# Differential attention's scores: from four products over 128 rows to three products over 64 rows for each map

## The chip, the cores and the metric

The kernel runs on one core of one Trainium2 chip. The metric is the device time of one execution in microseconds; the time before is the median of three runs. The core has five engines that work beside each other and meet at semaphores: TensorE (PE; the profile shows its weight loads apart, as PEld), VectorE (DVE), ScalarE (ACT), GpSimd (POOL) and SyncE (SP), whose queue issues nearly all DMA transfers here.

## The reference

One decoder layer over 1024 positions with a width of 1024: a norm, one wide projection (7184 columns), then two groups of heads side by side, eight of differential softmax attention and four of gated linear attention (GLA), then an output projection over both, a norm and the residual. All of it is float32. What the change touches is the first half of the differential attention:

```python
q = q * (DA_HEAD_DIM ** -0.5)                      # (B, S, 8 heads, 2 maps, 64)
s = jnp.einsum('bqhmd,bkhmd->bhmqk', qb, k)        # scores of two maps, each over 64 dimensions
mask = key_pos[None, :] <= q_pos[:, None]
p = jax.nn.softmax(jnp.where(mask, s, -jnp.inf), axis=-1)
w = p[:, :, 0] - lam * p[:, :, 1]
return jnp.einsum('bhqk,bkhv->bqhv', w, v)
```

A head has two maps, each with queries and keys of 64 dimensions; the weights are the difference of the two softmaxes, and the values have 128 dimensions.

## The kernel before

**Numbers in two parts.** Matrix products run on float32r operands, which keep fewer bits than float32. To hold the precision, an operand is split into a part rounded to float32r (hi) and the rest (lo), and a product is made of hi·hi, lo·hi and hi·lo. So most products in the kernel are three matmuls into one accumulation in PSUM, and each matmul (`mm`, L116) loads its own stationary operand. PE keeps the order in which the kernel writes matmuls and transposes (`keep_in_program_order`); a scheduler places the work of the other engines.

**Stages.** The input projection (`go`, `step`, L540 and L367) runs over pairs of column blocks with a seven-product scheme; GLA's work is fed in between (`fill`). Each finished block of 128 columns by 512 positions goes through `take` (L303), which splits q and k of a head into hi and lo (`qk_st`) and stores them in DRAM (L318). From about 650 us on three streams are merged (`merge`, L895 and L1290): the scores of all heads (`all_scores`, L991), the values (`all_values`, L1094) and the early part of the output projection (`out_early`, L1166, tiles `ypart`). Each stream gives each step a cost, and `merge` writes next the step of the stream that is furthest behind its line; so the order of matmuls on PE in this stage is fixed when the kernel is built. The last 60 us or so finish the output projection (`yps`).

**Scores before.** In DRAM, q and k of a head lie as `[map, part, 64, S]`. `load_qk` (L811) brings one half of the positions into an SBUF tile whose 128 rows are the 64 dimensions of the hi part above the 64 of the lo part, the two maps beside each other in the columns. For k there is a second tile, `ks`, with the parts swapped. A matmul of q with k over all 128 rows then gives hi·hi + lo·lo, and one of q with ks gives lo·hi + hi·lo: two matmuls make all four products of one map. `scores` (L944) does this for a block of 128 queries, for each map and for each part of up to 512 keys (`parts_of`, L922): `sc` is one of three PSUM banks, used in turn (`sc_bank`, L933); DVE reads it, adds the mask and keeps the minimum (L967; q is stored negated, so the minimum stands for the maximum); ACT takes the exponential (L975). After the second map DVE and POOL combine the two (L980 to L984). Blocks of queries go from the last to the first, so block 7 needs all keys and block 0 only 128 of them (a matmul has at least 256 columns).

**Loads before.** The tiles of the next head are loaded in the midst of a head (after block 4: the second half of q, both halves of k and ks) and at its end (the first half of q). The second halves have one buffer each, in which all heads follow each other; the first halves of k and ks alternate between two.

**Values.** `values` (L1006) turns the weights with PE transposes (`wtr`), splits them in two (`wt_hi`, `wt_lo`) and multiplies them with v (`po`).

Of the kernel before, what the change touches and what calls it, by code (L numbers as in the profile page):

```python
# [20 lines left out]
DA_HEADS = 8  # L21
# [10 lines left out]
def hymba_kernel(  # L32
# [50 lines left out]
    lam = const.tile([P, 1], F32, name="lam")  # L83
# [1 line left out]


    qk_d = {
        n: [tc.dram_tile([2, 2, 64, S], F32, name=f"{n}{h}_d") for h in range(DA_HEADS)]
        for n in "qk"
    }  # L90
    v_d = [tc.dram_tile([2, P, NT, P], F32, name=f"v{h}_d") for h in range(DA_HEADS)]
# [12 lines left out]
    def bank(i, shape, name):  # L104
        return psum.tile(shape, F32, tag=f"b{i}", name=name)
# [10 lines left out]
    def mm(*a, **k):  # L116
        tc.keep_in_program_order(pe.matmul(*a, **k))  # L117
# [35 lines left out]
    kp = ctx.enter_context(tc.tile_pool(name="kp", bufs=1))  # L153
# [39 lines left out]
    y, z = len(pairs) - 2, len(pairs) - 1  # L193
# [109 lines left out]
    def take(kind, n, half, unit, c):  # L303

        cs = cols(half)
        if kind in ("QA", "KA"):
            h = n + unit

            ending = made[0] > len(order) - LEAD
            tag, bufs = ("raw", 4) if ending and order[made[0] - 1][1] == 7 else ("st", 2)  # L310
            st = ap.tile([P, 2, 512], F32R, tag=tag, name="qk_st", bufs=bufs)
# [1 line left out]
            act.activation(st[:, 0], c, AF.Copy, scale=scale)  # L313
            dve.scalar_tensor_tensor(st[:, 1], c, scale, fp(st[:, 0]), ALU.mult, ALU.subtract)
            d = qk_d["q" if kind == "QA" else "k"][h]
            for m in range(2):
                rows = slice(64 * m, 64 * m + 64)
                ins = sp.dma_start(d[m, :, :, cs].rearrange("t p s -> p t s"), fp(st[rows]))  # L318
                if ending:
                    tc.keep_in_program_order(ins)  # L320
        elif kind == "VA":

            def sink(pt):
# [15 lines left out]
        elif kind in ("GA", "GB"):  # L339
# [5 lines left out]
            d = g_d[n + unit] if kind == "GA" else gg_d[n][unit]  # L345
            sp.dma_start(d[:, cs], g)
        elif kind == "QB":
            g = n + unit
            e_q, _ = decs[g]
            q = ap.tile([P, 2, 512], F32, tag="st", name="gq_st", bufs=2)  # L350
# [481 lines left out]
    for _ in fill[0] if fill else ():  # L832
        pass
    fill.clear()
    for n in ("q", "k", "ks"):
        load_qk(0, n, 1)
        if n != "q":
            load_qk(0, n, 0)
    load_qk(0, "q", 0)

    E, wo = D // P, {}
    md = mixd.rearrange("(e p) s -> p e s", p=P)
# [79 lines left out]
    def parts_of(n):  # L922
        return [(0, max(n, 256))] if n <= 512 else [(0, 512), (512, max(n, 768))]
# [9 lines left out]
    def sc_bank(name, shape):  # L933
        n_sc[0] += 1
        return bank(SC[n_sc[0] % 3], shape, name)
# [6 lines left out]
    w, used, scored = {}, set(), []  # L942

    def scores(h, qb):  # L944

        n = (qb + 1) * P
        qc = slice(qb % 4 * P, qb % 4 * P + P)
        st = const.tile([P, 6], F32, tag="stt", name="stt", bufs=4)
        p0 = pp.tile([P, n], F32, tag=f"p0_{qb}", name="p0", bufs=1)
        p1 = smp.tile([P, S], F32, tag="p1", name="p1", bufs=2)  # L950
        for m, p in enumerate((p0, p1)):
            q = qk[h, "q", qb // 4][:, m, qc]
            parts = parts_of(n)
            for i, (a, b) in enumerate(parts):
                sc = sc_bank("sc", [P, 512])
                for j, name in enumerate(("k", "ks")):
                    for half in range(2):
                        lo, hi = max(a, half * 512), min(b, half * 512 + 512)
                        if lo < hi:
                            mm(  # L960
                                sc[:, lo - a : hi - a], q,
                                qk[h, name, half][:, m, lo - half * 512 : hi - half * 512],
                                start=(j == 0), stop=(j == 1),
                            )
                e = min(b, n)
                last = i == len(parts) - 1
                dve.tensor_tensor_reduce(  # L967
                    p[:, a:e], sc[:, : e - a],
                    maskt[:, NZ + P - (e - a) :] if last else maskt[:, : e - a],
                    1.0, 3e38 if i == 0 else st[:, 4 + m : 5 + m], ALU.add, ALU.min,  # L970
                    st[:, m : m + 1] if last else st[:, 4 + m : 5 + m],
                )
# [6 lines left out]
                if last and m:  # L979
                    dve.reciprocal(st[:, 4:6], st[:, 2:4])  # L980
                    pool.tensor_scalar(  # L981
                        p1[:, :n], p1[:, :n], st[:, 5:6], lam, ALU.mult, ALU.mult
                    )
                    dve.scalar_tensor_tensor(  # L984
                        p0[:, :n], p0[:, :n], st[:, 4:5], p1[:, :n], ALU.mult, ALU.subtract
                    )
                    w[h, qb] = p0
                    c += 0.25 + n / 1024 * 1.4
                yield c

    def all_scores():  # L991
        for h in range(DA_HEADS):
            for qb in range(NT - 1, -1, -1):
                if qb % 2 and h:
                    yield lambda h=h, qb=qb: (h - 1, qb // 2) in used
                yield from scores(h, qb)
                if qb == 4 and h + 1 < DA_HEADS:
                    for n in ("q", "k", "ks"):
# [276 lines left out]
    def last_times(st, dh, part, e):  # L1275
# [8 lines left out]
    T = 8 * 36.0  # L1284
    LAG = 21.0
    s_cost = sum(
        2 * sum(0.08 + (min(b, n) - a) / 512 * 0.56 for a, b in parts_of(n)) + 0.25 + n / 1024 * 1.4
        for n in range(P, S + 1, P)
    )
    merge(  # L1290
# [119 lines left out]
```

## Time and profile before

| | us |
|---|---|
| median of three runs | 1022.69 |
| lowest, highest | 1018.75, 1025.47 |
| the profiled execution | 1019.5 |
| its span, first to last instruction | 1017.8 |
| mean granted TensorE clock | 0.997 |

The profile is of one execution. A group's row gives source line, engine, operation and the tiles (out<-in), the shape, the count, then busy time in us, the mean ns of one record, and the idle time of the engine just ahead of the group, with what ended it. All matmuls are written by the helper at L117 and all transposes by the one at L120, so they are told apart by their tiles: `sc` scores, `po` values, `wtr` turned weights, `ypart` and `yps` the output projection, `x`, `y`, `z` the input projection. Matmuls are pipelined, and the end of a matmul's record is modelled; starts are what to compare. SPq is the queue of SP, where DMA transfers are issued.

### The profile page before, as it was taken

The page shows a single profiled execution, that of the slowest core. Times are in us where ns is not written, and L with a number is a line of the kernel's source. Part 1 is how long each engine was busy: PE and PEld are TensorE (multiplying, and loading weights), DVE is VectorE, ACT ScalarE, POOL GpSimd, SP SyncE. Part 2 cuts the span into 40 slices and gives each one's busy share as a digit, 9 for nine tenths or more (in the row PEclk, how much of TensorE's full clock was granted, in tenths as well). Part 3 has the DMA queues.
Part 4 walks back from the last instruction along what each step waited for, and adds up shares of the span by engine and source line. Part 5 has one row for each costly group of instructions (what it writes and reads, how often), then busy time and mean ns, then how long its engine had stood idle before and what let it go on. Part 6 is the DMA issues. An engine that isn't in the chain of part 4 may idle for free.

```text
span 1017.8 us, 15017 instructions
## 1 busy us (share of the span) xinstructions
PE 981.8 (96%) x5006; PEld 823.2 (81%) x5006; DVE 727.6 (71%) x1486; ACT 606.1 (60%) x1208; POOL 133.2 (13%) x148
## 2 busy tenths in 40 slices
PE   4999999999999999999999999999999999999997
PEld 3777888887888878888888888778888887888765
DVE  5897866887667857867767765577777777777645
ACT  7754633684366635645567654356666667777664
POOL 6200000000001001000000000021231222343222
PEclk9999999999999999999999999999999999999999
DMA  9432435556867888888776647896566579975667
GB/s 333 153 87 87 136 123 189 181 173 223 258 226 240 259 258 273 273 281 267 247 254 193 189 155 250 280 368 222 185 217 195 198 268 374 273 187 82 164 192 149
DMA packets 145581, 220.39 MB, mean 217 GB/s; under 512 B 15216, under 2 KB 70512, under 8 KB 145408
## 3 DMA queue, kind: packets, MB, share of 16 engines
q1 hardware_dynamic: 141472, 212.09, 64.0%
q0 software_dynamic: 4032, 7.34, 4.8%
q8 instruction: 39, 0.64, 0.3%
q14 instruction: 38, 0.31, 0.1%
HBM read 133.93 MB, written 88.60 MB: 219 GB/s over the span
## 4 chain that ended last, share of the span: by engine, by line
PE 73%; DMA 10%; DVE 8%; issue 3%; ACT 2%; SPq 2%; POOL 0%; DVEq 0%; ACTq 0%
PE x L117 17%; PE z L117 11%; PE y L117 11%; PE ypart L117 10%; PE sc L117 5%; PE po L117 5%; PE yps L117 4%; DMA wo_d<-wo_raw 4%; PE wtr L120 2%; PE gpo L117 2%; DMA wo_raw<-in_w_out_dram 2%; DMA q_d<-qk_st 1%; DMA wo_hi<-wo_d 1%; PE vtr L120 1%; DVE w L259 1%
## 5 line engine op out<-in xcount | busy, mean ns | idle before, releaser
L975 ACT ACTIVATE p<-p,stt 128x896 f32<-128x896 f32 (+7 forms) x128 | 99.5, 777 | 49.4 <-DVE stt L967 44.6
L117 PE MATMUL y<-h_hi,w 128*128 128x512 f32 x448 | 114.0, 396 | 1.9 <-DVE s L510 1.0
L117 PE MATMUL x<-s_hi,w 128*128 128x512 f32 x448 | 112.5, 394 | 1.4 <-ACT s L373 1.4
L117 PE MATMUL z<-s_hi,w 128*128 128x512 f32 x448 | 113.6, 396 | 0.2 <-ACT s L373 0.2
L373 ACT COPY s<-x 128x512 f32<-128x512 f32 x84 | 49.0, 583 | 101.9 <-PE x L117 100.4
L258 ACT CAST w<-t 128x512 fp32r<-128x512 f32 x112 | 68.9, 621 | 62.0 <-PE y L117 30.1
L259 DVE TENSOR_TENSOR w<-t,w 128x512 fp32r<-128x512 f32 x112 | 76.6, 687 | 32.1 <-ACT w L258 31.6
L117 PEld LDWEIGHTS y<-h_hi,w 128*128 128x128 f32 x448 | 82.6, 188 | 19.4 <-ACT h_hi L466 2.1
L117 PEld LDWEIGHTS x<-s_hi,w 128*128 128x128 f32 x448 | 83.0, 188 | 18.6 <-ACT s L373 2.1
L117 PEld LDWEIGHTS z<-s_hi,w 128*128 128x128 f32 x448 | 82.4, 188 | 16.9 <-ACT s L373 0.6
L967 DVE CUSTOM_DVE_ANT_0 p<-sc,maskt 128x512 f32<-128x512 f32 (+3 forms) x128 | 74.8, 586 | 29.5 <-PE sc L117 28.5
L981 POOL TENSOR_SCALAR p<-p,stt,lam 128x1024 f32<-128x1024 f32 (+3 forms) x64 | 54.6, 854 | 277.4 <-DVE stt L980 155.2
L117 PE MATMUL ypart<-wo_hi,m_hi 128*128 128x512 f32 x192 | 79.6, 414 | 0.9 <-ACT yst L1163 0.8
L259 DVE TENSOR_TENSOR w<-w_raw,w 128x512 fp32r<-128x512 f32 x78 | 54.9, 704 | 32.6 <-ACT w L258 32.4
L117 PE MATMUL ypart<-wo_hi,m_lo 128*128 128x512 f32 x192 | 75.7, 394 | 0.0
L117 PE MATMUL ypart<-wo_lo,m_hi 128*128 128x512 f32 x192 | 75.5, 393 | 0.0
L729 POOL TENSOR_SCALAR_AFFINE_SELECT gan<-gan 128x512 f32<-128x512 f32 x8 | 10.7, 1336 | 484.1 <-ACT gan L728 484.1
L117 PE MATMUL sc<-k,q 128*128 128x512 f32 (+1 forms) x192 | 70.3, 369 | 1.9 <-DVE stt L967 1.9
L117 PE MATMUL sc<-ks,q 128*128 128x512 f32 (+1 forms) x192 | 66.2, 347 | 0.0
L258 ACT CAST w<-w_raw 128x512 fp32r<-128x512 f32 x78 | 48.1, 618 | 30.2 <-PE y L117 15.3
L384 DVE TENSOR_TENSOR c<-z,s 128x512 f32<-128x512 f32 x56 | 38.6, 688 | 35.6 <-ACT s L373 28.1
L984 DVE SCALAR_TENSOR_TENSOR p<-p,stt,p 128x1024 f32<-128x1024 f32 (+3 forms) x64 | 52.2, 816 | 16.1 <-POOL p L981 15.7
(202 smaller groups left out, 2250.5 us busy)
## 6 DMA issues: line engine op xcount, KB each, us to landing
w_raw<-in_w_in_dram SPq DMA_DIRECT2D x56, 512.0 KB, 5.5
wo_raw<-in_w_out_dram SPq DMA_DIRECT2D x32, 256.0 KB, 3.3
v_d<-v_st SPq DMA_DIRECT2D x32, 256.0 KB, 2.5
wo_d<-wo_hi SPq DMA_DIRECT2D x32, 256.0 KB, 2.4
wo_d<-wo_raw SPq DMA_DIRECT2D x32, 256.0 KB, 4.5
k_d<-qk_st SPq DMA_DIRECT2D x32, 256.0 KB, 4.5
q_d<-qk_st SPq DMA_DIRECT2D x32, 256.0 KB, 5.3
q<-q_d SPq DMA_DIRECT2D x32, 256.0 KB, 5.4
```

The costliest lines, as they stand in the source:

```text
L117: tc.keep_in_program_order(pe.matmul(*a, **k))
L120: tc.keep_in_program_order(pe.transpose(dst, src, ident))
L258: act.copy(w[:, 0], src)
L259: dve.tensor_tensor(w[:, 1], src, fp(w[:, 0]), ALU.subtract)
L373: act.copy(b[k], ps)
L384: dve.tensor_tensor(c, p0, p1, ALU.add)
L729: pool.affine_select(a, a, [[0, 4], [1, P]], ALU.is_ge, 0.0, base=0, channel_multiplier=-1)
L967: dve.tensor_tensor_reduce(p[:, a:e], sc[:, : e - a], maskt[:, NZ + P - (e - a) :] if last else maskt[:, : e - a], 1.0, 3e38 if i == 0 els ...
L975: act.activation(p[:, :n], p[:, :n], AF.Exp, bias=st[:, m : m + 1], scale=-1.0, accum_out=st[:, 2 + m : 3 + m],)
L981: pool.tensor_scalar(p1[:, :n], p1[:, :n], st[:, 5:6], lam, ALU.mult, ALU.mult)
L984: dve.scalar_tensor_tensor(p0[:, :n], p0[:, :n], st[:, 4:5], p1[:, :n], ALU.mult, ALU.subtract)
```

## The change

q and k lie in DRAM as `[part, 128, S]`: 64 rows of the first map above 64 rows of the second, with hi and lo apart, so that `take` stores a block with one transfer in place of two. In SBUF a tile has the two maps in the two halves of its rows and the two parts beside each other in the columns; the swapped tile `ks` is gone. A score is made of three matmuls with a contraction over 64 rows (hi·hi, lo·hi, hi·lo; lo·lo is left out), for both maps in turn, the first map on rows 0 to 63 and the second on rows 64 to 127, into two PSUM banks at once; then DVE reads the two banks. Each q and k tile is loaded with one transfer. Even heads use one set of four buffers and odd heads another, and all loads of the next head are issued after block 6, the second block of a head. The costs that `merge` goes by change with it: a step is now one part of both maps.

```diff
@@ take
-            for m in range(2):
-                rows = slice(64 * m, 64 * m + 64)
-                ins = sp.dma_start(d[m, :, :, cs].rearrange("t p s -> p t s"), fp(st[rows]))
-                if ending:
-                    tc.keep_in_program_order(ins)
+            ins = sp.dma_start(d[:, :, cs].rearrange("t p s -> p t s"), fp(st))
+            if ending:
+                tc.keep_in_program_order(ins)
@@ load_qk
-        if h % 2 and half == 0 and n != "q":
-            t = smps[0].tile([P, 2, 512], F32R, tag=f"{n}0", name=f"{n}0")
+        if h % 2 == 0:
+            t = kp.tile([P, 2, 512], F32R, tag=f"{n}{half}", name=f"{n}{half}")
+        elif n == "k":
+            t = kp.tile([P, 2, 512], F32R, tag=f"ks{half}", name=f"k{half}")
         else:
-            t = kp.tile([P, 2, 512], F32R, tag=f"{n}{half}", name=f"{n}{half}")
-        for m in range(2):
-            d = qk_d["q" if n == "q" else "k"][h][m, :, :, cols(half)]
-            if n != "ks":
-                sp.dma_start(fp(t[:, m]), d.rearrange("t p s -> (t p) s"))
-            else:
-                for i in range(2):
-                    sp.dma_start(fp(t[64 * i : 64 * i + 64, m]), d[1 - i])
+            t = smps[0].tile([P, 2, 512], F32R, tag=f"q{half}", name=f"q{half}")
+        sp.dma_start(fp(t), qk_d[n][h][:, :, cols(half)].rearrange("t p s -> p t s"))
@@ scores
-        for m, p in enumerate((p0, p1)):
-            q = qk[h, "q", qb // 4][:, m, qc]
-            parts = parts_of(n)
-            for i, (a, b) in enumerate(parts):
-                sc = sc_bank("sc", [P, 512])
-                for j, name in enumerate(("k", "ks")):
-                    for half in range(2):
-                        lo, hi = max(a, half * 512), min(b, half * 512 + 512)
-                        if lo < hi:
-                            mm(
-                                sc[:, lo - a : hi - a], q,
-                                qk[h, name, half][:, m, lo - half * 512 : hi - half * 512],
-                                start=(j == 0), stop=(j == 1),
-                            )
+        q = qk[h, "q", qb // 4]
+        parts = parts_of(n)
+        for i, (a, b) in enumerate(parts):
+            k, k0 = qk[h, "k", a // 512], a // 512 * 512
...
+            scs = [sc_bank("sc", [P, 512]) for _ in range(2)]
+            for j, (x, y) in enumerate(((0, 0), (1, 0), (0, 1))):
+                for m, sc in enumerate(scs):
+                    rows = slice(64 * m, 64 * m + 64)
+                    mm(
+                        sc[:, : b - a], q[rows, x, qc], k[rows, y, a - k0 : b - k0],
+                        start=(j == 0), stop=(j == 2),
+                    )
+            for m, (p, sc) in enumerate(zip((p0, p1), scs)):
                 dve.tensor_tensor_reduce(
...
-                c = 0.08 + (e - a) / 512 * 0.56
...
+            c = 0.16 + (e - a) / 512 * 0.9
@@ all_scores
-                if qb == 4 and h + 1 < DA_HEADS:
-                    for n in ("q", "k", "ks"):
-                        load_qk(h + 1, n, 1)
-                    for n in ("k", "ks"):
-                        load_qk(h + 1, n, 0)
-            if h + 1 < DA_HEADS:
-                load_qk(h + 1, "q", 0)
+                if qb == 6 and h + 1 < DA_HEADS:
+                    for n, half in (("q", 1), ("k", 0), ("k", 1), ("q", 0)):
+                        load_qk(h + 1, n, half)
```

More of the change, by code (lines that the diff above doesn't have):

```diff
@@ L87, in hymba_kernel @@
     qk_d = {
-        n: [tc.dram_tile([2, 2, 64, S], F32, name=f"{n}{h}_d") for h in range(DA_HEADS)]
+        n: [tc.dram_tile([2, P, S], F32, name=f"{n}{h}_d") for h in range(DA_HEADS)]
         for n in "qk"
@@ L834, in hymba_kernel @@
     fill.clear()
-    for n in ("q", "k", "ks"):
[L836 to L839, printed above, removed]
+    for n, half in (("q", 1), ("k", 0), ("k", 1), ("q", 0)):
+        load_qk(0, n, half)
     E, wo = D // P, {}
@@ L978, in scores @@
                     )
[L979 to L989, printed above, removed]
+            c = 0.16 + (e - a) / 512 * 0.9
+            if last:
+                dve.reciprocal(st[:, 4:6], st[:, 2:4])
+                pool.tensor_scalar(p1[:, :n], p1[:, :n], st[:, 5:6], lam, ALU.mult, ALU.mult)
+                dve.scalar_tensor_tensor(
+                    p0[:, :n], p0[:, :n], st[:, 4:5], p1[:, :n], ALU.mult, ALU.subtract
+                )
+                w[h, qb] = p0
+                c += 0.25 + n / 1024 * 1.4
+            yield c
     def all_scores():
@@ L996, in all_scores @@
                 yield from scores(h, qb)
-                if qb == 4 and h + 1 < DA_HEADS:
-                    for n in ("q", "k", "ks"):
-                        load_qk(h + 1, n, 1)
-                    for n in ("k", "ks"):
-                        load_qk(h + 1, n, 0)
-            if h + 1 < DA_HEADS:
-                load_qk(h + 1, "q", 0)
+                if qb == 6 and h + 1 < DA_HEADS:
+                    for n, half in (("q", 1), ("k", 0), ("k", 1), ("q", 0)):
+                        load_qk(h + 1, n, half)
         scored.append(True)
@@ L1286, in hymba_kernel @@
     s_cost = sum(
-        2 * sum(0.08 + (min(b, n) - a) / 512 * 0.56 for a, b in parts_of(n)) + 0.25 + n / 1024 * 1.4
+        sum(0.16 + (min(b, n) - a) / 512 * 0.9 for a, b in parts_of(n)) + 0.25 + n / 1024 * 1.4
         for n in range(P, S + 1, P)
```

4 lines of the change are left out of this document (2 added, 2 removed).

## The prediction

> **What bounds the kernel now.** I read the page from the top: busy time, the slices, then the chain that ended last.
>
> ```profile
> PE 981.8 (96%) x5006; PEld 823.2 (81%) x5006; DVE 727.6 (71%) x1486; ACT 606.1 (60%) x1208; POOL 133.2 (13%) x148
> PE   4999999999999999999999999999999999999997
> PE 73%; DMA 10%; DVE 8%; issue 3%; ACT 2%; SPq 2%; POOL 0%; DVEq 0%; ACTq 0%
> ```
>
> TensorE is busy for 96% of the span, in all slices but the first and the last, and holds 73% of the chain. A busy share says little of matmuls that overlap, so next I cut the stage that the change touches into windows (columns: window, length, then busy time of PE, weight loads, DVE, ACT and POOL, granted clock, DMA share, GB/s).
>
> ```profile
> 650.00:670.00 20.00, 17.71 (x82) 13.76 (x81) 14.12 (x38) 8.73 (x16) 3.27 (x3) 1.00 1.00 371
> 700.00:750.00 50.00, 49.87 (x292) 43.33 (x291) 37.40 (x103) 34.78 (x75) 12.00 (x13) 1.00 0.66 209
> 950.00:1018.00 68.00, 57.31 (x279) 46.21 (x277) 33.98 (x100) 38.37 (x108) 16.30 (x19) 0.98 0.68 167
> ```
>
> In the middle of the score stage PE has work for 49.87 of 50 us at the full clock, and DVE, the next, for 37.40: a microsecond taken from PE's stream there is a microsecond off the end. In the first 20 us the DMA engines are full (share 1.00), and in the last 68 PE waits for others.
>
> How many score matmuls there are, by shape (columns: operation, tile of the array, moving columns, count, busy us, ns of one record):
>
> ```profile
> L117 PE MATMUL sc<-k,q 128*128 128x512 f32 x96 | 40.1, 418 | 0.0
> L117 PE MATMUL sc<-ks,q 128*128 128x512 f32 x96 | 37.8, 393 | 0.0
> L117 PE MATMUL sc<-k,q 128*128 128x256 f32 x64 | 19.2, 302 | 0.5 <-DVE stt L967 0.5
> L117 PE MATMUL sc<-ks,q 128*128 128x256 f32 x64 | 17.9, 282 | 0.0
> L117 PE MATMUL sc<-k,q 128*128 128x384 f32 x32 | 11.4, 356 | 1.4 <-DVE stt L967 1.4
> L117 PE MATMUL sc<-ks,q 128*128 128x384 f32 x32 | 10.8, 338 | 0.0
> ```
>
> A record of 393 ns is not what a matmul costs: records overlap. The timeline gives the pitch, from one start to the next.
>
> ```profile
> 705.19 0.40 PE L117 MATMUL sc<-k,q 128*128 128x512 f32 x1
> 705.42 0.39 PE L117 MATMUL sc<-ks,q 128*128 128x512 f32 x1
> 705.65 0.39 PE L117 MATMUL ypart<-wo_hi,m_hi 128*128 128x512 f32 x1
> ...
> 716.46 0.33 PE L117 MATMUL sc<-k,q 128*128 128x384 f32 x1
> 716.63 0.34 PE L117 MATMUL sc<-ks,q 128*128 128x384 f32 x1
> 716.81 0.39 PE L117 MATMUL ypart<-wo_hi,m_hi 128*128 128x512 f32 x1
> ...
> 719.14 0.28 PE L117 MATMUL sc<-k,q 128*128 128x256 f32 x1
> 719.26 0.28 PE L117 MATMUL sc<-ks,q 128*128 128x256 f32 x1
> 719.38 0.40 PE L117 MATMUL po<-wt_hi,v 128*128 128x256 f32 x2
> ```
>
> So 0.23 us for 512 columns, 0.175 for 384, 0.12 for 256, and scores now take 192 x 0.23 + 64 x 0.175 + 128 x 0.12 = 44.2 + 11.2 + 15.4 = 70.8 us of PE's stream.
>
> **Part 1, the matmuls.** Two matmuls per map and part, over 128 rows, become three per map over 64 rows: 576 in 288 pairs (144 of 512 columns, 48 of 384, 96 of 256). Nothing in the trace uses half the rows, so the cost has two bounds. If the two of a pair stream together, a pair costs one pitch: 144 x 0.23 + 48 x 0.175 + 96 x 0.12 = 33.1 + 8.4 + 11.5 = 53.0 us, 17.8 less than now. If they stream one after the other, it is 106.0 us, 35.2 more. I take the first: the halves share no row, no weights and no PSUM bank, the order puts the two maps next to each other, and a record of 0.39 us beside a pitch of 0.23 shows that the array already holds two matmuls at once. But that is an argument and no measurement, and I keep both ends.
>
> The Trainium skill, "TensorE: Matmul & The Clock Gate", Part 3 on packing small matmuls, says that matmuls on different row groups run concurrently, their starts some 4 ns apart. No run here shows it yet; by it the 288 pairs would take, as an estimate, 1.2 us above the lower bound.
>
> **Part 2, weight loads.** Each of the 576 loads its own weights. Two rows bound a load's cost: short matmuls in a stream, and records of loads of 128 and of 64 columns.
>
> ```profile
> 399.82 1.78 PE gpo L117 x16
> ...
> L117 PEld LDWEIGHTS sc<-ks,q 128*128 128x128 f32 x192 | 36.4, 190 | 4.4
> ...
> L117 PEld LDWEIGHTS gkl_ps<-h_lo,wl 128*64 128x64 f32 x12 | 1.6, 135 | 1.2
> ```
>
> Sixteen matmuls of 128 columns take 1.78 us, 0.11 each; 64 more columns of weights take 190 - 135 = 55 ns, so 128 take 0.11: a load occupies its path for 0.11 us whatever streams. A pair needs two, 0.22 us one behind the other. That hides under 0.23, but not under 0.175 or 0.12. If the halves load side by side it costs nothing; if not, 144 narrower pairs take 0.22 and the sum is 33.1 + 31.7 = 64.8. I take nothing, since the halves have weight rows of their own, and keep +11.8 as the other end. The second matmul of a group can start behind the first by up to a load (0.11) or by nothing; once per group of six that is 0 to 10.6 us in 96 groups. I take 0.03, 2.9 us.
>
> **Part 3, changes of geometry.** In the built order of the changed kernel the score matmuls stand in 95 runs, with full-array matmuls between: 190 changes between 128 and 64 rows. The nearest rows are the low-rank product, which goes from 128 to 64 columns of the array in the midst of a stream.
>
> ```profile
> 77.88 0.62 PE L117 MATMUL z<-s_lo,w 128*128 128x512 f32 x2
> 78.33 0.85 PE L117 MATMUL gkl_ps<-s_hi,wl 128*64 128x512 f32 x3
> ...
> 81.33 0.85 PE L117 MATMUL gkl_ps<-h_lo,wl 128*64 128x512 f32 x3
> 82.01 0.63 PE L117 MATMUL z<-s_hi,w 128*128 128x512 f32 x2
> ```
>
> The last z starts at about 77.88 + 0.62 - 0.39 = 78.11 and the first gkl_ps 0.22 later; back at the end, 81.79 to 82.01, again 0.22. That is the plain pitch, so I take 0. The upper end is the array running empty, 0.39 - 0.23 = 0.16 us each, 30.4 us. The Trainium skill, "TensorEngine Tiling (Array Packing)", Key Properties, speaks against the change: a switch of tiling mode drains TensorE. The trace does not agree for columns (0.22 against a pitch of 0.23); for rows no run shows it. It is a rival below.
>
> **Part 4, PSUM banks.** Three banks rotate. A group now fills two at once, and DVE reads them one after the other.
>
> ```profile
> PE sc L117 <- DVE stt L967: 1.9, 2, 1.4
> L967 DVE CUSTOM_DVE_ANT_0 p<-sc,maskt 128x512 f32<-128x512 f32 (+3 forms) x128 | 74.8, 586 | 29.5 <-PE sc L117 28.5
> ```
>
> Now PE waits 1.9 us in all. With the pitches above laid along the built orders, before 3 reuses of a bank come less than 2 us of PE work after its last matmul; in the changed order 30 do, most at 1.3. A read takes 0.59 us, two 1.17, and DVE reads in its own order behind other work, so perhaps every third of the 30 is late by some 0.3 us: 3 us. PE takes its work in order: behind a score matmul that waits stand the ypart, wtr and po matmuls, and behind those the copies of ACT and DVE that empty them. Ends: 0, and 15 (each late by one read, 30 x 0.5). DVE and ACT do the same reads and exponentials as before.
>
> **Part 5, transfers.**
>
> ```profile
> L120 PE MATMUL vtr<-ident,c 128*128 128x128 f32 x128 | 18.3, 277 | 3.0 <-DVE c L384 3.0
> ...
> 358.83 6.13 DMA q_d<-qk_st
> 654.98 7.33 DMA q_d<-qk_st
> 662.37 9.48 DMA v<-v_d
> ...
> q<-q_d SPq DMA_DIRECT2D x32, 256.0 KB, 5.4
> k<-k_d SPq DMA_DIRECT2D x32, 256.0 KB, 5.8
> ks<-k_d SPq DMA_DIRECT2D x64, 128.0 KB, 6.1
> ```
>
> The ks loads go (64 x 128 KB = 8.4 MB of 220), and 128 load issues on SP become 32, 64 stores 32; the bytes stored stay. All of this lies beside a full PE but where the chain names a transfer: the q_d store at 358.83, and the q_d and v transfers at 655 to 672, with the DMA engines full. Loads a head earlier need no wait on SP, since their buffers were last read a head before; the v loads queue behind fewer of them. The stores cost SP issue time alone, beside a full PE. I take 2 us gained; ends 0 and 5, the second all that PE idles from 650 to 670 (20 - 17.71 = 2.3) and ahead of the vtr transposes (3.0, if that wait behind DVE's c is the store's at 358.83, whose buffer the next tile needs).
>
> **The sum**, against the profiled execution of 1019.5 us (span 1017.8): -17.8 + 0 + 2.9 + 0 + 3 - 2 = -13.9, so 1005.6. That execution lies 3.2 under the median of the runs, 1022.7; the forecast on that is 1009.
>
> **Rivals.**
> - *Pairs overlap, loads do not.* +11.8 on the sum: -2.1, so 1021. For it: 0.11 us per load in every stream shown. Against: separate rows.
> - *Each change of geometry drains the array.* Slower, from a point: 13.9 / 190 = 0.073 us per change. At 0.16 it is -13.9 + 30.4 = +16.5, 1039. For it: 190 changes, almost none adjacent. Against: the 0.22 of the low-rank product.
> - *The change does not do what it says:* the halves do not stream together. +35.2 on the matmuls, +3 for banks, -2 for transfers: +36, 1059; as PE is full, all of it lands on the end. For it: no row shows two streams in one array.
>
> **Chances.** Forecast 0.36 (its own range 1003 to 1013), loads in series 0.20, drain 0.19, no overlap 0.25. A measurement of this kernel tells about 1% (10 us) from no change. Faster by over 1%: nearly all of the forecast and the mild end of the drain, 0.36. Within 1%: loads in series, and the middle of the drain, 0.27. Slower: no overlap and the full drain, 0.37. The range reaches from 1003 to 1062, past the no-overlap case; only combinations of rivals lie above.
>
> **What would show it.** Starts of the two maps' score matmuls some 0.03 us apart and pairs 0.23 apart confirm part 1; single starts 0.23 apart refute it. Pairs of 256 columns at 0.12 or 0.22 settle part 2. The step into and out of a score run, above the pitch, settles part 3. The row of PE sc waiting for DVE stt should stay under 15 us, and ks gone from the list of DMA issues without PE waiting for q or k. The prediction is wrong above all if PE's time in the scores' stream rises instead of falling.

## The result, and the profile after

| | before | after |
|---|---|---|
| median, us | 1020.72 (4 runs, 1018.37 to 1025.47) | 1036.16 (4 runs, 1035.40 to 1037.17) |
| profiled execution | 1019.5 | 1036.62 |
| its span | 1017.8 | 1034.9 |

The ratio is 1.0146, with a 95% interval of 1.0104 to 1.0188: the changed kernel is 15 us slower, where the forecast was 1009. The time lies in the range and close to the rival in which each change of geometry drains the array (1039).

The page of the kernel after, its busy times and its chain of waits:

```profile
PE 1000.8 (97%) x5198; PEld 801.9 (77%) x5198; DVE 727.2 (70%) x1486; ACT 604.2 (58%) x1208; POOL 137.0 (13%) x148
PE 83%; DVE 6%; DMA 4%; ACT 4%; issue 3%; POOL 0%; DVEq 0%; SPq 0%; POOLq 0%; ACTq 0%
```

PE is busy for 19 us more (1000.8 against 981.8), the span is 17.1 us longer, and PE's part of the chain has grown from 73% to 83%. So the time was lost in PE's own work more than in waits for others; what it waited for comes further down. Next, where: the stage from the first score to the first `yps`, as one window, of the kernel before and of the kernel after (columns as in the prediction).

```profile
652.00:954.00 302.00, 295.26 (x1698) 254.57 (x1696) 226.77 (x622) 206.70 (x457) 85.97 (x92) 1.00 0.75 234
```

```profile
647.00:971.00 324.00, 316.68 (x1893) 235.89 (x1892) 227.66 (x624) 205.46 (x459) 85.10 (x92) 0.99 0.61 190
```

The windows are rounded to whole microseconds; by the starts themselves the stage went from 302.2 us (652.0 to 954.2) to 323.2 (647.7 to 970.9). It begins 4.3 us earlier and takes 21.0 longer, and what follows it takes 0.4 longer: 17.1 together. In it DVE, ACT and POOL do the same work in the same time, and only PE does more. The DMA share falls, as `ks` is gone.

What the score matmuls and their loads look like now (groups by shape, columns as before):

```profile
L117 PE MATMUL sc<-k,q 64*128 64x512 f32 x288 | 46.6, 427 | 0.0
L117 PE MATMUL sc<-k,q 64*128 64x256 f32 x192 | 20.7, 317 | 4.4 <-DVE stt L958 4.4
L117 PE MATMUL sc<-k,q 64*128 64x384 f32 x96 | 13.2, 371 | 0.0
L117 PE MATMUL ypart<-wo_hi,m_hi 128*128 128x512 f32 x192 | 88.4, 460 | 0.1
L117 PEld LDWEIGHTS sc<-k,q 64*128 64x128 f32 x576 | 45.1, 186 | 33.2 <-issue 19.5 <-DVE stt L958 6.4 <-DVE p L973 1.5
```

In the kernel before, the `ypart` row was this:

```profile
L117 PE MATMUL ypart<-wo_hi,m_hi 128*128 128x512 f32 x192 | 79.6, 414 | 0.9 <-ACT yst L1163 0.8
```

Two things stand out. A matmul that the diff does not touch, the first of each `ypart` group, has become 46 ns longer on average; it is often the one that follows the scores. And the loads of the scores have 33.2 us of idle time ahead of them, of which 19.5 is "issue": time in which nothing that the profile shows held them up. The timeline of PE around one group of scores shows why (start, us, then the operation; x6 is one row for six matmuls):

```profile
671.74 0.28 PE L117 MATMUL po<-wt_lo,v 128*128 128x256 f32 x1
671.95 0.96 PE L117 MATMUL sc<-k,q 64*128 64x512 f32 x6
672.84 0.50 PE L117 MATMUL ypart<-wo_hi,m_hi 128*128 128x512 f32 x1
673.18 0.39 PE L117 MATMUL ypart<-wo_hi,m_lo 128*128 128x512 f32 x1
673.41 0.39 PE L117 MATMUL ypart<-wo_lo,m_hi 128*128 128x512 f32 x1
...
720.17 0.28 PE L117 MATMUL po<-wt_lo,v 128*128 128x256 f32 x1
720.38 0.63 PE L117 MATMUL sc<-k,q 64*128 64x256 f32 x6
720.93 0.50 PE L117 MATMUL ypart<-wo_hi,m_hi 128*128 128x512 f32 x1
721.27 0.39 PE L117 MATMUL ypart<-wo_hi,m_lo 128*128 128x512 f32 x1
```

Six matmuls of 512 columns end 0.96 us after the first start. One after the other they would take 5 x 0.23 + 0.39 = 1.54, so the two maps do overlap. But the `po` ahead of them has 256 columns, and the scores start 0.21 us behind it where 0.12 is the pitch. At the end the same: `ypart` follows, and the `ypart` behind that comes 0.34 us later, where 0.23 is the pitch; its record has 0.50 us, not 0.39. The weight loads of the same stretch say what happened (the last bracket is the idle time ahead of the load, and what ended it):

```profile
671.95 0.53 PEld L117 LDWEIGHTS sc<-k,q 64*128 64x128 f32 x6
672.84 0.19 PEld L117 LDWEIGHTS ypart<-wo_hi,m_hi 128*128 128x128 f32 x1 [0.36 <-issue]
672.95 0.19 PEld L117 LDWEIGHTS ypart<-wo_hi,m_lo 128*128 128x128 f32 x1
673.18 0.19 PEld L117 LDWEIGHTS ypart<-wo_lo,m_hi 128*128 128x128 f32 x1
```

In a plain stream a load starts one matmul ahead: that of the `ypart` at 673.41 starts at 673.18. At the two changes, at 671.95 and at 672.84, the load starts together with its own matmul. Nothing was fetched ahead across the change, and the 0.11 us of the load lies open.

The starts in nanoseconds, which the timeline rounds, give the four steps of this group (worked out from the trace's records):

```
start, us   step, us   pitch of the one ahead   over
671.738                                                po, 256 columns
671.949     0.211      0.12                     0.09   scores, first pair (second map 4 ns later)
672.287     0.338      0.23                     0.11   second pair (3 ns)
672.523     0.236      0.23                     0      third pair (3 ns)
672.842     0.319      0.23                     0.09   ypart
673.179     0.337      0.23                     0.11   ypart
673.409     0.230      0.23                     0      ypart
```

So each change of geometry costs twice: the next matmul starts about 0.09 us late, and the one behind it 0.11 later still, because the load was not hidden. Summed over all 190 changes, against those pitches: late starts 9.15 us going in and 8.90 coming out (medians 0.094 and 0.093); open loads 10.23 going in, and coming out 7.89 for 71 matmuls and 1.3 for the 24 places where a `wtr` transpose follows (0.055 each). Together 37.5 us, or 0.197 per change. A run of scores has two changes and costs 0.40 us; a group of 512 columns saves one pitch of 0.23 by the overlap, one of 256 saves 0.12.

What PE waited for, over the whole span, in the two rows that changed (total in us, times, longest), and what DVE did before the score matmuls could go on:

```profile
PE sc L117 <- DVE stt L958: 4.4, 1, 4.4
...
PE vtr L120 <- DVE c L382: 0.8, 1, 0.8
```

```profile
660.38 0.17 DVE L971 RECIPROCAL stt<-stt 128x2 f32<-128x2 f32 x1 [1.69 <-ACT p L965]
661.76 1.15 DVE L973 SCALAR_TENSOR_TENSOR p<-p,stt,p 128x896 f32<-128x896 f32 x1 [1.22 <-POOL p L972]
```

The wait for a bank is a single one of 4.4 us, from 659.2 to 663.6 near the start of the stage, 2.5 more than before. DVE was not busy through it: it stood idle for 1.69 us behind ACT's exponentials and for 1.22 behind POOL, and read the next scores only after that, at 662.83. Over the whole stage PE waited for 7.2 us, against 6.6 before: the other waits became shorter.

The granted clock changed too. The trace has it at half speed from 663.5 to 666.9 and from 858.1 to 861.5, which loses 1.7 us each time, 3.4 in all; in the kernel before it was full through the whole stage, but at half from 367.2 to 370.6, just behind the `vtr` wait.

The 4.3 us by which the scores start earlier are then 2.2 from that `vtr` wait behind `c` (3.0 before, 0.8 now) and 1.7 from the clock behind it, which stayed full here. Part of this belongs to the one execution that was profiled. In three further traces with the work ahead of the stage all but unchanged (the runs with 64 rows or 64 columns below) the first score starts at 650.9, 651.0 and 650.1, and 652.0 in the kernel before; in the eight traces with single stores (this kernel, its five variants and the two runs of transfers below) it starts between 647.5 and 649.2. The means, 651.0 and 648.2, are 2.8 apart.

For the stage: -17.8 (overlap) + 37.5 (changes) + 0.6 (all waits of PE) + 3.4 (clock) = +23.7, and 21.0 were measured. Some of the clock's loss stands in the 37.5 as well, as the steps at changes in those two stretches are longer (up to 0.36 us over the pitch); the rest of the 2.7 was not found.

### The profile page after: what moved, and what is told of

Same layout as the page of the kernel before. It is cut to its first block, busy times and chain, and to the rows that moved or that the text cites. A ratio compares the mean times of both kernels' runs of the same rounds, so it can differ in the third digit from the quotient of the medians.

```text
span 1034.9 us, 15212 instructions
## 1 busy us (share of the span) xinstructions
PE 1000.8 (97%) x5198; PEld 801.9 (77%) x5198; DVE 727.2 (70%) x1486; ACT 604.2 (58%) x1208; POOL 137.0 (13%) x148
## 4 chain that ended last, share of the span: by engine, by line
PE 83%; DVE 6%; DMA 4%; ACT 4%; issue 3%; POOL 0%; DVEq 0%; SPq 0%; POOLq 0%; ACTq 0%
PE x L117 19%; PE ypart L117 13%; PE z L117 13%; PE y L117 12%; PE sc L117 6%; PE po L117 5%; PE yps L117 4%; PE wtr L120 3%; PE gpo L117 3%; DMA wo_d<-wo_raw 1%; PE kv L117 1%; PE vtr L120 1%; PE ms L117 1%; PE gkl_ps L117 1%; DVE s_lo L491 1%
## 5 line engine op out<-in xcount | busy, mean ns | idle before, releaser
L117 PEld LDWEIGHTS y<-h_hi,w 128*128 128x128 f32 x448 | 82.5, 188 | 19.5 <-ACT h_hi L464 2.1
L117 PE MATMUL ypart<-wo_hi,m_hi 128*128 128x512 f32 x192 | 88.4, 460 | 0.1
L117 PE MATMUL sc<-k,q 64*128 64x512 f32 (+2 forms) x576 | 80.1, 381 | 4.4 <-DVE stt L958 4.4
L958 DVE CUSTOM_DVE_ANT_0 p<-sc,maskt 128x512 f32<-128x512 f32 (+3 forms) x128 | 70.6, 585 | 14.6 <-PE sc L117 14.0
L727 POOL TENSOR_SCALAR_AFFINE_SELECT gan<-gan 128x512 f32<-128x512 f32 x8 | 14.8, 1845 | 476.6 <-ACT gan L726 476.6
L117 PEld LDWEIGHTS sc<-k,q 64*128 64x128 f32 x576 | 45.1, 186 | 33.2 <-issue 19.5
L1007 DVE TENSOR_TENSOR wt_lo<-wtr,wt_hi 128x512 fp32r<-128x512 f32 (+1 forms) x80 | 50.6, 634 | 23.3 <-ACT wt_hi L1006 23.0
```

The source lines that it names most:

```text
L727: pool.affine_select(a, a, [[0, 4], [1, P]], ALU.is_ge, 0.0, base=0, channel_multiplier=-1)
L958: dve.tensor_tensor_reduce(p[:, a:e], sc[:, : e - a], maskt[:, NZ + P - (e - a) :] if last else maskt[:, : e - a], 1.0, 3e38 if i == 0 els ...
L1007: dve.tensor_tensor(lo[:, :n], pt[:, :n], fp(hi[:, :n]), ALU.subtract)
```

## The experiments

Times are medians, and ratios are against the kernel before on the same chip. Two theories were at hand. By the first, a change between 128 and 64 rows has a price of about 0.2 us. By the second, the two banks that are filled at once, or the loads of the halves, hold PE up.

**Full rows in the changed kernel.** The six score matmuls of a group go over all 128 rows; order, banks and loads are those of the changed kernel.

```diff
-                    rows = slice(64 * m, 64 * m + 64)
+                    rows = slice(0, P)
```

> The changed kernel with its six score matmuls per group taken over all 128 rows instead of one half each, in the same order, with the same banks, loads and reads; both maps then get the sum of the two maps' scores, so the output is not the reference's. No matmul changes the geometry of the array any more, and none overlaps another. Theory 1 (each change between 128 and 64 rows costs about 0.2 us, 190 of them 37.5 us, and the halves overlap fully): the overlap is lost, +53, the changes are saved, -37.5, so about 1052 us (1046 to 1057), starts 0.23 us apart, and the first matmul of a score run starts on the plain pitch. Rival (the halves cost nothing to enter and leave, and the loss comes from two banks filled at once or from the order): only the overlap is lost, +53, about 1089 us.

Measured: 1046.94 us (1046.27 to 1048.15), ratio 1.0263 (1.0233 to 1.0292). That is 10.8 more than the changed kernel. Without the overlap 288 pitches come on top, 53.0 us by the prediction's count; the bank wait falls from 4.4 to 0.4. What the missing changes gave back is then 53.0 - 4.0 - 10.8 = 38.2 us, 0.20 for each of 190. The clock was full throughout this stage; without the 3.4 us that it cost the changed kernel there, it is 34.8 us, 0.18 for each. The 1089 that holds if changes cost nothing (1036 + 53) is refuted. The starts agree:

```profile
678.74 0.28 PE L117 MATMUL po<-wt_lo,v 128*128 128x256 f32 x1
678.86 0.88 PE L117 MATMUL sc<-k,q 128*128 128x256 f32 x6
679.58 0.40 PE L117 MATMUL ypart<-wo_hi,m_hi 128*128 128x512 f32 x1
```

The scores start 0.12 us behind `po`, the plain pitch, and `ypart` 0.72 later, which is six pitches of 0.12 and nothing more. The total alone gives only the difference of two unknowns, the overlap lost and the changes saved; the starts, here and in the changed kernel, give each of them.

**More and shorter runs.** The three pairs of a group may be separated by other streams, so that 95 runs become 171.

```diff
+                if j < 2:
+                    yield (b - a) / 512 * 0.3
...
-            c = 0.16 + (e - a) / 512 * 0.9
+            c = 0.16 + (e - a) / 512 * 0.3
```

> The changed kernel with a step of the merge after each of the three pairs of a group, so that other streams' matmuls come between the pairs: 171 score runs in the built order instead of 95, 342 changes of geometry instead of 190; the same matmuls, loads and reads. Theory 1 (0.2 us per change): +152 x 0.197 = +30, about 1066 us (1060 to 1073), a few more if banks held longer make PE wait. Rival (no price per change): the same matmuls in another order, 1036 us within 5.

Measured: 1101.76 us (1101.44 to 1101.79), ratio 1.0798 (1.0767 to 1.0829): the direction is right and the size, 66 us over the changed kernel, twice what was expected. The waits and the clock of this run give the rest:

```profile
PE sc L117 <- DVE stt L960: 16.3, 14, 4.4
PE po L117 <- DVE wt_lo L1009: 4.7, 6, 2.5
PE yps L117 <- DVE stt L960: 4.0, 1, 4.0
```

```profile
core 0: 1100.0 us, clock 0.984
```

The 152 further changes cost 30 us at 0.197. The waits are 12, 4 and 3 us longer than in the changed kernel; that a bank is now held over other work would explain it, and was not tried. Up to PE's last matmul the trace has the clock at half for 30.7 us, against 6.8 in the changed kernel, so it lost 12 us more. That makes 61 of 66 us. The run speaks for the price but moved three things at once.

**One map after the other.** The three products of the first map are written ahead of the three of the second, so that neighbours in PE's order share their rows.

```diff
-            for j, (x, y) in enumerate(((0, 0), (1, 0), (0, 1))):
-                for m, sc in enumerate(scs):
+            for m, sc in enumerate(scs):
+                for j, (x, y) in enumerate(((0, 0), (1, 0), (0, 1))):
```

> The changed kernel with the three products of the first map ahead of the three of the second, in place of alternating; the same matmuls, the same 95 runs. If matmuls start in order and only neighbours in the order can overlap, the third of the first map and the first of the second overlap and the rest do not: five pitches in place of three, +2/3 x 53 = +35, about 1071 us. If the two halves run independently of the order: 1036 us. Neither theory of the changes of geometry is touched by this run; it says what the alternation is worth.

Measured: 1042.19 us (1041.62 to 1044.33), ratio 1.0219 (1.0189 to 1.0249). It is 6 us over the changed kernel, and far from 1071. PE's timeline:

```profile
683.74 0.39 PE L117 MATMUL ypart<-wo_lo,m_hi 128*128 128x512 f32 x1
684.06 0.63 PE L117 MATMUL sc<-k,q 64*128 64x256 f32 x6
684.62 0.66 PE L120 MATMUL wtr<-ident,p 128*128 128x128 f32 x4
```

The six still take 0.63 us, as in the changed kernel at 720.38. The six starts are at 684.060, .070, .284, .294, .401 and .411. The trace does not name the map of a matmul; as the starts come in pairs 10 ns apart at the pitch of 256 columns, the first of each pair is taken for the first map and the second for the second map. Read so, the second map's first matmul starts 10 ns behind the first map's, although two matmuls of the first map that stand ahead of it in the order start 0.22 and 0.34 us later. So which half comes first in the order does not decide the overlap. Two stretches of lower clock account for the time over the changed kernel:

```profile
660.00:680.00 20.00, 16.14 (x80) 11.61 (x81) 11.99 (x34) 8.85 (x22) 3.70 (x4) 0.83 0.90 330
960.00:980.00 20.00, 17.56 (x84) 13.63 (x81) 12.77 (x34) 13.36 (x35) 6.64 (x8) 0.75 0.44 105
```

In them the clock was at half for 6.8 and 10.2 us, a loss of 8.5 us; the changed kernel lost 3.4 in its two stretches. The difference, 5.1, is that of the two profiled executions (1041.75 and 1036.62). Both stretches stand behind waits of PE: 4.2 us for a score bank at 659.5, and two of 0.5 and 0.8 us from 968.0 on, with a further one of 1.2 us in the second stretch.

**A fourth bank for the scores.** The transposes give up one of their two banks.

```diff
-    SC, TR, PO, Y = order_b[:3], order_b[3:5], order_b[5], order_b[6:]
+    SC, TR, PO, Y = order_b[:4], order_b[4:5] * 2, order_b[5], order_b[6:]
...
-        return bank(SC[n_sc[0] % 3], shape, name)
+        return bank(SC[n_sc[0] % 4], shape, name)
```

> The changed kernel with four PSUM banks for scores in place of three, the fourth taken from the turned weights, which have one left in place of two; the order of work is as it was, 95 score runs. It measures the price of that exchange alone, as the base of the next run. Bank theory (two banks filled at once out of three cost the time): with four the wait of the score matmuls goes and the time falls well below 1036. Theory 1: the 4.4 us wait of the score matmuls goes, and the transposes wait for the one bank's readers, 80 times up to 1.2 us, so 1036 to 1090, with the waits of wtr in the profile saying how much.

Measured: 1054.83 us (1052.94 to 1056.78), ratio 1.0337 (1.0310 to 1.0363). The waits:

```profile
PE wtr L120 <- DVE wt_lo L1007: 11.2, 11, 2.2
PE wtr L120 <- ACT r L1056: 7.5, 6, 1.5
PE sc L117 <- DVE stt L958: 2.8, 2, 2.6
```

The scores' wait shrinks by 1.6 us, and the transposes, with one bank, wait 18.7, where the changed kernel has no such wait; this kernel is 18.7 us slower than the changed one (1054.83 - 1036.16), and that the two figures agree to the tenth is chance. With a fourth bank the scores still wait 2.8 us, and all they waited in the changed kernel was 4.4: a shortage of score banks was no large part of the loss.

**Longer runs.** On top of the four banks, all parts of a block of queries are one run, and blocks 3 and 2, and 1 and 0, share one: 48 runs in place of 95.

```diff
-            for qb in range(NT - 1, -1, -1):
...
-                yield from scores(h, qb)
+            for qbs in ((7,), (6,), (5,), (4,), (3, 2), (1, 0)):
...
+                yield from scores(h, qbs)
```

> Four banks for scores as in the run before it, and score matmuls in longer runs: all parts of a block of queries next to each other, and blocks 3 and 2, and 1 and 0, as one run; 48 runs and 96 changes of geometry in place of 95 and 190, the same matmuls. Theory 1: 94 changes fewer at 0.197 us, 18.5 us less than the run with four banks and the old order (the steps are coarser, so waits of other streams may give some of it back). Rival (changes of geometry cost nothing): the same as that run.

Measured: 1065.98 us (1065.09 to 1069.05), ratio 1.0457 (1.0433 to 1.0482): 11 us more than with four banks and 95 runs, where 18.5 less were expected. The price per change stayed (medians 0.093 for the late start and 0.106 for the open load going in), so some 19 us of changes are gone. But the coarser steps bunch the transposes on their one bank:

```profile
PE wtr L120 <- DVE wt_lo L1014: 22.3, 24, 1.7
PE wtr L120 <- ACT r L1063: 12.1, 6, 3.0
PE po L117 <- ACT wt_hi L1013: 3.5, 5, 0.8
```

These are 37.9 us against 19.4 (the first two, and 0.7 of `po` behind `wt_hi`): 18.5 more, which eats the gain. Of the 11 us beyond that, 1.7 are the clock (half for 3.4 us more in the stage), and the last stage takes 2.1 us longer; the rest was not found. As a way to a better kernel it failed, and as a test of the total it settles nothing.

**The price by itself.** Here the kernel before is kept, with its order on PE. In every second `ypart` group the third product uses 64 of its 128 rows: 96 matmuls with full ones on both sides, 192 changes, no overlap and no new wait for a bank.

```diff
+            r = slice(0, 64) if i == 2 and dh == 0 else slice(0, P)
             mm(
-                ps, a[:, e - e0, :], b[:, cols(dh)],
+                ps, a[r, e - e0, :], b[r, cols(dh)],
```

> The kernel before, with 96 of its ypart matmuls (the third product, left half of the columns) taken over rows 0 to 63 of the array alone, which leaves the other half of that small product out of the output projection. Scores, loads, banks and the order on PE are those of before; 192 changes between 128 and 64 rows come in, and no overlap. Theory 1: 192 x 0.197 = +38 us, about 1059 (1053 to 1065), with the start behind a change 0.09 late and the first matmul after it 0.106 longer, as in the changed kernel. Rival (the price in the changed kernel belongs to its pairs, banks or waits): the time of before, 1021.

Measured: 1052.36 us (1052.13 to 1053.63), ratio 1.0330 (1.0300 to 1.0359), the kernel before 1019.59: 32.8 us more, 0.171 per change. That is just under the lower end of what was expected (1053), and far from 1021. PE's timeline at one of the matmuls:

```profile
672.48 0.39 PE L117 MATMUL ypart<-wo_hi,m_hi 128*128 128x512 f32 x1
672.71 0.40 PE L117 MATMUL ypart<-wo_hi,m_lo 128*128 128x512 f32 x1
673.04 0.50 PE L117 MATMUL ypart<-wo_lo,m_hi 64*128 64x512 f32 x1
673.47 0.50 PE L117 MATMUL ypart<-wo_hi,m_hi 128*128 128x512 f32 x1
673.80 0.40 PE L117 MATMUL ypart<-wo_hi,m_lo 128*128 128x512 f32 x1
```

The steps are 0.23, 0.33, 0.43 and 0.33: late by 0.10 going in, by 0.10 for the open load and 0.09 coming out, and by 0.11 for the next open load. That is the same pattern as at the scores, in a kernel that has nothing else of the change. No two matmuls run side by side here, so neither banks nor the side-by-side loads are needed to explain it.

**Half as many.**

```diff
+            r = slice(0, 64) if i == 2 and dh == 0 and e % 2 == 0 else slice(0, P)
```

> As the run before it with 48 such matmuls, 96 changes. Theory 1: +19 us, about 1040 (1036 to 1044), half of that run's loss. Rival: 1021; or, if the loss is not in proportion to the changes, anything but half.

Measured: 1033.82 us (1032.51 to 1037.52), ratio 1.0141 (1.0106 to 1.0175): 14.2 us for 96 changes, 6 under what was expected and below its range. From this run to the one above, 96 further changes cost 18.5 us, 0.193 each. By the steps of all of them in the traces, each changed matmul costs 0.39 us, so 19 and 37 us; in both runs 4 to 5 us of that did not reach the end. With 96 such matmuls, PE's waits in the stage went from 6.6 to 4.3 us, which takes up half; for the other half, and for the run with 48, it stays open.

**Columns in place of rows.** 80 of the same matmuls use 64 columns of the array and all rows: 160 changes.

```diff
+            r = slice(0, 64) if i == 2 and dh == 0 and e != last else slice(0, P)
             mm(
-                ps, a[:, e - e0, :], b[:, cols(dh)],
+                ps[r], a[:, e - e0, r], b[:, cols(dh)],
```

> The kernel before, with 80 of the same ypart matmuls taken over 64 columns of the array in place of 128 (all rows; half of the output rows do without that product): 160 changes between 128 and 64 columns. The prediction took such a change, seen at the low-rank product, as the nearest row for a change of rows. If a change of columns costs nothing: the time of before, 1021 within 4. If any change of geometry drains the array: 160 x 0.197 = +32, about 1053.

Measured: 1019.35 us, the median of ten executions, of which one took 2535.14 us and is not in the ratio; ratio 1.0002 (0.9983 to 1.0020): nothing. The timeline has the plain pitch going in and coming out, and records of 0.39:

```profile
650.79 0.39 PE L117 MATMUL ypart<-wo_hi,m_lo 128*128 128x512 f32 x1
651.02 0.39 PE L117 MATMUL ypart<-wo_lo,m_hi 128*64 128x512 f32 x1
651.25 0.40 PE L117 MATMUL ypart<-wo_hi,m_hi 128*128 128x512 f32 x1
```

So the row that the prediction took for the price, a change of columns, was read rightly and was of the wrong kind. The Trainium skill, "TensorEngine Tiling (Array Packing)", Key Properties, says that a change of tiling mode drains TensorE. For rows the trace agrees, with 0.2 us per change; for columns it does not, with a ratio of 1.0002 over 160 changes.

**The transfers by themselves.** In the kernel before, `take` stores a block with one transfer, and the loads follow the new layout; the matmuls stay. In a first form all loads of `q` and `k` became two transfers each.

```diff
-            for m in range(2):
-                rows = slice(64 * m, 64 * m + 64)
-                ins = sp.dma_start(d[m, :, :, cs].rearrange("t p s -> p t s"), fp(st[rows]))
-                if ending:
-                    tc.keep_in_program_order(ins)
+            ins = sp.dma_start(d[:, :, cs].rearrange("t p s -> p t s"), fp(st))
...
-                sp.dma_start(fp(t[:, m]), d.rearrange("t p s -> (t p) s"))
...
+            for i in range(2):
+                sp.dma_start(fp(t[64 * i : 64 * i + 64, m]), d[1 - i if n == "ks" else i])
```

> The kernel before with one change alone taken over: q and k blocks stored with one transfer over 128 rows in place of two over 64, with the layout in DRAM that goes with it; loads of q and k then take two transfers of 64 rows each, as those of ks do already. Scores as before. If the 4 us by which the changed kernel starts its first score matmul earlier come from these stores: about 4 us less than before, 1017 to 1018. If they come from the order of the other transfers: no difference, or some us more for the 64 added issues on SP.

Measured: 1027.59 us (1026.10 to 1028.59), ratio 1.0072 (1.0046 to 1.0099). The first score came 4.3 us earlier, at 647.7, as in the changed kernel. But 8 us were lost at one place further on, on PE and on ACT:

```profile
867.93 1.23 ACT L1158 COPY yst<-ypart 128x512 f32<-128x512 f32 x2 [5.78 <-DMA y_d<-yst]
868.57 0.80 PE L117 MATMUL ypart<-wo_hi,m_hi 128*128 128x512 f32 x1 [8.34 <-ACT yst L1158]
```

`ypart` needs its bank emptied by ACT, ACT needs the `yst` buffer stored, and the store had stood behind the doubled loads in SP's queue: it was issued at 860.91, behind loads of `k` and `ks` issued from 854.01 on. After the wait the clock was at half for 6.8 us, 3.4 more. In a second form the parts of a row lie side by side in DRAM, so that the loads of `q` and `k` stay as many as before.

```diff
-                ins = sp.dma_start(d[m, :, :, cs].rearrange("t p s -> p t s"), fp(st[rows]))
+            ins = sp.dma_start(d[:, :, cs], fp(st))
...
-                sp.dma_start(fp(t[:, m]), d.rearrange("t p s -> (t p) s"))
+                sp.dma_start(fp(t[:, m]), d.rearrange("p t s -> (p t) s"))
...
-                    sp.dma_start(fp(t[64 * i : 64 * i + 64, m]), d[1 - i])
+                    sp.dma_start(fp(t[i::2, m]), d[:, 1 - i])
```

> The kernel before with the stores of q and k in one transfer each, as in e5, but with rows laid out so that q and k are still loaded with one transfer per map (parts alternate row by row in the tile; ks takes every second row); the count of load issues is that of before. If the 8 us wait late in e5 came of its added issues on SP, and its earlier start of the scores of the single stores: 3 to 4 us less than before, about 1016. If any new layout upsets the order of transfers: about e5's 1027.

Measured: 1018.24 us (12 runs, 1015.83 to 1022.76) against 1021.09 (16 runs), ratio 0.9973 (0.9953 to 0.9992). That is 2.9 us less, at the edge of what was expected. The first score starts at 647.5, 4.5 us earlier than in the trace of before; the stage takes 304.6 us, 2.4 more, of which 1.7 are a stretch of half clock (666.1 to 669.5) behind a wait of 1.9 us. The `ypart` wait of 8.3 us is 0.8 here, as in the kernel before, which fits the doubled loads as its cause; the layout differs as well. It is the one version that beats both kernels, by 0.3%.

## Why the prediction was wrong, and where it was right

- **What bounds the kernel** was read rightly: PE is full in the score stage, and what was added to its stream landed on the end nearly whole (21.0 us of 23.7).
- **Part 1** was right: the maps start 2 to 4 ns apart, and the pairs run at the plain pitch. With full rows the pairs take two pitches, and the time rises although the changes are saved.
- **Part 2** was right that the loads go side by side: the six loads of a group of 256 columns do not stretch it (0.63 us at 720.38), which refutes the rival of loads in series. The stagger of 0.03 per group was too high: at 4 ns for 96 groups it is 0.4 us in place of 2.9.
- **Part 3** is the step that failed: "That is the plain pitch, so I take 0." The row was that of a change of columns, and a change of columns does cost nothing; a change of rows costs 0.197 us, 37.5 for 190. The upper end, 0.16, was too low as well. It thought of the array running empty and not of the weight load, which was not fetched ahead at the changes and lies open for another 0.11. The prediction named the point from which this turns the sign (0.073), and gave the rival that has half of the mechanism, the late start, only 0.19. That this rival's 1039 lies so near the time measured is partly luck: its price was 7 us too low, and its terms for stagger, banks and transfers erred by 5 us the other way.
- **Part 4** had the size (2.5 us for 3) by luck and not the form: not many reuses late by a little, but one wait of 4.4 us near the start of the stage, while PE's other waits shrank. It also left out the clock, which fell to half behind that wait.
- **Part 5** had 2 us for 4.3 in the profiled pair, at the place it named: the store ahead of the `vtr` transposes. Over all traces the stage starts 2.8 us earlier with single stores, and the kernel before with that store alone gained 2.9 us, so this part holds without the rest of the change and was closer than the 4.3 suggests.
- **The sum again**, with what was measured: -17.8 + 0 + 0.4 + 37.5 + 2.5 - 4.3 = +18.3, so 1037.8 against 1036.62 of the profiled execution. It leaves out what partly cancels: the clock in the stage (+3.4, some of it in the 37.5) and the waits of PE that became shorter (-1.9).

## What to carry to other kernels

Two half-height products overlapped fully here, but each run of them paid about 0.4 us for going in and coming out, so count the runs in the built order before: here a run would have had to hold some 1.7 groups of 512 columns to pay, and nearly all held one. A row of the trace prices only the operation it shows: a change of columns said nothing about a change of rows, and when the nearest row is of another kind, the point from which the unknown cost turns the sign deserves more weight than that row. And the stores in fewer, larger transfers could be had by themselves here, for 0.3%, as long as the loads were not split in return. Last, a wait of PE may cost more than its length: look at the granted clock behind it before a sum is called closed.

## What the hardware showed unexpectedly

- No weight load was fetched ahead across a change between 128 and 64 rows, in either direction: at 671.95 and 672.84 the load starts with its matmul, and the median step behind a change is 0.106 us over the pitch on both sides.
- PE started matmuls of the second half of the rows ahead of waiting ones of the first half that stood before them in the order (10 ns against 0.22 and 0.34 us), if the starts are given to the maps as above. The Trainium skill, "TensorE: Matmul & The Clock Gate", Part 3, says that matmuls keep the program's order in start and end; for two halves of the rows this trace does not agree.
- The granted clock fell to half behind waits of PE of a few microseconds. After the 4.4 us wait for a score bank the kernel after ran at half from 663.5 to 666.9, which the window below shows as 0.66, and the pitch of `ypart` of 512 columns grew to 0.43 us in it. The twelve traces have ten waits of PE of 2.28 us or more from 40 us on, and each has such a fall, beginning 2.1 to 4.7 us after the wait does. The eleven other falls that came before PE's last matmul stand behind shorter waits, of 0.96 to 2.11 us or a few close together, but many waits of that length have none: one of 1.12 us at 854.7 in the kernel after has one, one of 2.19 at 928.2 in the run with four banks has not. A fall lasted 3.4 us or two or three times that. No run made a wait on purpose, so that the waits are the cause is read from this agreement alone.

```profile
662.00:667.00 5.00, 3.42 (x11) 2.53 (x11) 3.18 (x10) 1.95 (x4) 0.00 (x0) 0.66 1.04 415
```

```profile
665.54 0.63 PE L117 MATMUL ypart<-wo_lo,m_hi 128*128 128x512 f32 x1
665.96 0.63 PE L117 MATMUL ypart<-wo_hi,m_hi 128*128 128x512 f32 x1
```
